# Later places for the steps between the products of a two-layer hybrid decoder, and the key latent's norm moved to GpSimd

## The chip, the cores and the metric

The kernel runs on one core of a Trainium2 chip. The metric is the device time of one execution in microseconds (us), as the median over several executions. Beside it stands one execution taken by the hardware profiler, from which all durations below come. The engines are TensorE (PE in the profile; PEld is its weight load), VectorE (DVE), ScalarE (ACT), GpSimd (POOL) and SyncE (SP), whose queue issues the DMAs. Each works through its own queue in order; semaphores tie the queues together.

## The reference

Two layers over 512 tokens of width 1024. In each, one projection of the normed input feeds three mixers side by side; their outputs are projected, gated, added and projected once more, and a squared-ReLU feed-forward of width 4096 follows. Cut to what matters here:

```python
# B: latent attention, 8 heads
q  = rmsnorm(cq, q_norm_g) @ w_uq           # query latent: 512 wide
kv = rmsnorm(ckv, kv_norm_g) @ w_ukv        # key latent: 256 wide
# A: chunked scan (4 chunks of 128 tokens), then a norm over each of 2 groups
y = ssd_chunked(xs * dt, dt * a, bm, cm) + d_skip * xs
y = rmsnorm((y * silu(z)).reshape(..., 2, 512), norm_g)
# C: gated delta rule, chunk after chunk
v_new = u - w @ state
o     = (q * exp(g)) @ state + attn @ v_new
state = state * exp(g_last) + (k * exp(g_last - g)).T @ v_new
```

`rmsnorm(x, g)` is `x * rsqrt(mean(x * x) + eps) * g`.

## The kernel before

**Products.** Nearly all the time goes into matrix products with both sides split into a high and a low part (`whi`/`wlo`, `xh`/`xl`), three matmuls for each pair of tiles (lines 200 to 202, `mm3`). ScalarE makes a weight's high part (L172), VectorE its low part (L173); the raw weights come by DMA into `wraw`, two buffers. `dense_F` (L204) gives outputs with features on the partitions: for each pair of k (128 rows of the weight each) it goes through the column tiles, and for each of them through the two k. A product over 1024 rows and 256 columns is 48 matmuls of 512 columns.

**Order.** The program is written down stage by stage, and a planner builds each engine's queue from it: what comes earlier in the program goes first when its inputs are ready by the planner's own costs. Two helpers bend that order on the matmul queue. `place` (L162) notes the last matmul of each k and column tile of a product under a key such as `((ly, "k", 2), 3, 0)`: product, k, column tile. `behind` (L155) makes an instruction follow the matmul noted under a key. It is a lower bound in the queue's order and no semaphore; the planner may still put the instruction later. With it the small matmuls and transposes of the mixers are laid between the matmuls of a big product that doesn't depend on them.

**The stages that the change touches**, in each of the two layers:

- *First stage and attention.* `front` (L397) computes the key latent `ck_tok` (four tiles of 128 tokens by 256), the rotary key and the step sizes. `query_latent` (L531) computes the query latent in two halves. `latent` (L509) squares the key latent on ScalarE, computes the factor (`rsq`, L276: one step on VectorE and a power on GpSimd, L278), scales the four tiles on VectorE (L519), transposes them on TensorE (L524) and splits them. It is called behind the second half, L565. The sums of the query latent's squares are matmuls with a column of ones (L568). Then for each pair of heads come the query product (four k, three column tiles: 36 matmuls, L600), the key and value products and the softmax.
- *Scan.* `ssd_group` (L734) runs for two groups over four chunks t: decays by DMA, L784 (within the chunk), L795 (from the state), L802 (state update), the squares' sums L816. At the end the norm's factors are transposed (L820), written to DRAM and read back on all partitions. These steps lie between matmuls of the attention's output product, with tag `(ly, 1, dp, "g")` for its gate half and `(ly, 1, dp, "y")` for the other.
- *Delta rule.* `gdn_unit` (L996) runs for two units u of four heads over four chunks t. For each t: L1044 (queries by keys), L1055 (keys by the state), L1058 on VectorE, L1061 (`pw`), L1066 on VectorE and L1072 on ScalarE, L1075 (`pS`, the state update), L1082, L1085 (`po`), L1092, the output norm (L1101 to L1113). At the end the output is transposed (L1118). Unit 0's steps lie between the matmuls of unit 1's query and value products (`(ly, "k", 2)`, `(ly, "v", 4)`, `(ly, "v", 6)`), unit 1's between those of the output projection. `pw_place`, `pg_place` and `end_place` (L1033 to L1035) hold the places. L1024 transposes a value tile behind its convolution.

PSUM has four banks for products (`acc`), three for small work (`sm`) and one more (`yt`).

Of the kernel before, what the change touches and what calls it, by code (L numbers as in the profile page):

```python
# [10 lines left out]
F32 = mybir.dt.float32  # L11
# [4 lines left out]
ALU = mybir.AluOpType  # L16
# [4 lines left out]
P = 128  # L21
# [34 lines left out]
def hybrid_kernel(ctx, tc, a, out, depth=2, taps=None):  # L56
# [326 lines left out]
    for ly in range(depth):  # L383
# [125 lines left out]
        def latent(pl, tok, width, gi, nm):  # L509

            nk = width // P
            ss = mk(sp, [P, T], F32, "lss")
            for t in range(T):
                jk = mk(ml, [P, width], F32, "pn3", 2)
                act.activation(jk, tok[t], AF.Square, accum_out=ss[:, t : t + 1])
            rs = mk(sp, [P, T], F32, "lrs")
            rsq(rs, ss, 1.0 / width, EPS)
            for t in range(T):
                dve.tensor_scalar(tok[t], tok[t], rs[:, t : t + 1], None, ALU.mult)  # L519
            hs, ls = hilo_tags(pl, nm, nk)  # L520
            for k in range(nk):
                ps = sm_bank()
                for t in range(T):
                    pe.transpose(ps[:, t * P : (t + 1) * P], tok[t][:, k * P : (k + 1) * P], ident)  # L524
                split_gain(hs[k], ls[k], ps, col(gi + k))
            return hs, ls
# [23 lines left out]

        query_latent(0)
# [15 lines left out]
        for t in range(T):  # L567
            pe.matmul(ps[:, t : t + 1], cq_sq[0][:, t * P : (t + 1) * P], ones[:, 0:1], start=True, stop=True)  # L568
# [13 lines left out]
        for hp in range(4):  # L582
# [17 lines left out]
            *pq, pp = dense_F(q_weights(), tiles(384), 512, cqh, cql)  # L600
# [133 lines left out]
        def ssd_group(g, yh, yl):  # L734
# [34 lines left out]
            for t in range(T):  # L769
# [11 lines left out]
                for c in range(4):  # L781
                    for i in range(2):
                        h = 2 * c + i
                        x = pe.matmul(py[64 * i : 64 * i + 64, c * P : (c + 1) * P], xd[:, t, h * 64 : (h + 1) * 64], e2[h // 4][:, h % 4, :], start=True, stop=True)  # L784
                        if t == 0:
                            behind(((ly, 1, 2 * g, "g"), 2, 0), x)
# [29 lines left out]
                pe.matmul(pss[:, t : t + 1], sq[:, 0], ones[:, 0:1], start=True, stop=True)  # L816
# [3 lines left out]
            behind(((ly, 1, 2 * g, "y"), 6, 0), pe.transpose(ps[:T, :P], rs, ident))  # L820
# [175 lines left out]
        def gdn_unit(u, kT, ork, cc, cd, Yt, yh, yl):  # L996
# [20 lines left out]
            for i in range(2):  # L1017
                for j, pj in enumerate(dense_F(weights(w_in, O_GV + (4 * u + 2 * i) * P, 256, D), tiles(256), D, xh, xl, tag=(ly, "v", 4 * u + 2 * i))):
                    h = 2 * i + j
                    vf = mk(br, [P, S], F32, "ft4", 2)  # L1020
                    gconv_silu(pj, 8 + 4 * u + h, vf)
                    ps = sm_bank()
                    for t in range(T):
                        pe.transpose(ps[:, t * P : (t + 1) * P], vf[:, t * P : (t + 1) * P], ident)  # L1024
                    dve.tensor_tensor(v[:, :, h * P : (h + 1) * P], ps.rearrange("p (t n) -> p t n", t=T),
                                      bc_last(ork[:, i, :], P), ALU.mult)
# [6 lines left out]
            pw_place = (seq[0], 3, 0), (seq[0], 5, 1), (seq[1], 1, 0)  # L1033
            pg_place = (seq[0], 5, 0), (seq[0], 7, 1)
            end_place = (seq[2], 1, 0) if u == 0 else (seq[2], 5, 0)  # L1035
            st = None
            for t in range(T):
# [30 lines left out]
                if t < T - 1:  # L1068
# [5 lines left out]
                    for i in range(2):  # L1074
                        pe.matmul(pS[:, i * 256 : (i + 1) * 256], ktok[i][:, t, :], vd[:, i * 256 : (i + 1) * 256], start=True, stop=True)  # L1075
# [8 lines left out]
                for h in range(4):  # L1084
                    x = pe.matmul(po[:, h * P : (h + 1) * P], pt_[:, h, :], vn[:, h * P : (h + 1) * P], start=True, stop=True)  # L1085
                    if t == T - 1:
                        behind((seq[1], 1, 1), x)
# [373 lines left out]
```

## Time and profile before

| | |
|---|---|
| median of 3 runs | 2291.31 us (2291.30 to 2293.06) |
| the profiled execution | 2290.89 us, of which the span from first to last instruction is 2289.1 us |
| PE busy | 2264.0 us, 99% of the span |
| DVE busy | 1647.4 us, 72% |
| ACT busy | 1202.8 us, 53% |
| POOL busy | 58.7 us, 3%, 75 instructions |
| DMA | 244.23 MB, 107 GB/s on the mean |
| clock granted to TensorE | 0.998 |

How to read the profile. A row of a group has line, engine, operation, tiles written and read, shapes and count, then its busy time, the mean of one in ns, and the idle time of its engine just before, with what ended it. A row of the order of time has its start in us from the span's start, its duration, engine, line and tiles; in square brackets is the idle time before it and what ended that. A row of the waits has who waited for whom, then idle time in total, times, and the longest. Matmuls overlap in the array, so a matmul's duration is longer than the distance to the next one's start.

### The profile page before, as it was taken

The numbers are of one execution on the slowest core, as the hardware profiler recorded it, in microseconds if no ns is written. First come the engines' busy times: TensorE is split into PE (matmuls) and PEld (weight loads), VectorE is DVE, ScalarE is ACT, GpSimd is POOL, SyncE is SP. The second block draws the span as 40 slices with busy tenths as digits, with TensorE's granted clock in tenths as the row PEclk, the third lists the DMA queues.
The fourth block names the chain that finished last, engine by engine and source line by source line (L and its number), as shares of the span: only waits on it lengthen the run. The fifth ranks groups of instructions, "written<-read, shape, count | busy, mean of one in ns | idle before, by whom it ended". The sixth has DMA issues, their size and how long they took to land.

```text
span 2289.1 us, 32304 instructions
## 1 busy us (share of the span) xinstructions
PE 2264.0 (99%) x11822; PEld 1866.7 (82%) x11822; DVE 1647.4 (72%) x3258; ACT 1202.8 (53%) x2508; POOL 58.7 (3%) x75
## 2 busy tenths in 40 slices
PE   9999999999999999999999999999999999999998
PEld 8888787888878888888888887878888887888886
DVE  7776567876676778767867775668757667778668
ACT  6766744333444465554657667443335435645545
POOL 0000000000000000000000000000001000000000
PEclk9999999999999999999999999999999999999999
DMA  4223633452225143233132236344422241432231
GB/s 144 81 74 102 193 102 120 123 150 76 77 74 172 59 148 111 92 109 105 52 100 78 77 104 199 96 119 140 129 76 82 65 170 52 166 108 99 89 111 47
DMA packets 220176, 244.23 MB, mean 107 GB/s; under 512 B 34272, under 2 KB 172528, under 8 KB 220016
## 3 DMA queue, kind: packets, MB, share of 16 engines
q1 hardware_dynamic: 220016, 242.16, 34.6%
q8 instruction: 93, 1.52, 0.3%
q14 instruction: 67, 0.55, 0.1%
HBM read 225.66 MB, written 11.74 MB: 104 GB/s over the span
## 4 chain that ended last, share of the span: by engine, by line
PE 91%; DVE 3%; ACT 2%; POOL 1%; DMA 1%; issue 0%; DVEq 0%; POOLq 0%; ACTq 0%; SPq 0%
PE acc L200 23%; PE acc L202 23%; PE acc L201 23%; PE sm L200 3%; PE sm L202 3%; PE sm L201 3%; DVE wlo L173 1%; PE sm L784 1%; PE sm L682 1%; PE sm L1085 1%; PE sm L1075 1%; PE yt L698 1%; ACT whi L172 1%; PE sm L662 1%; PE sm L659 0%
## 5 line engine op out<-in xcount | busy, mean ns | idle before, releaser
L173 DVE TENSOR_TENSOR wlo<-wraw,whi 128x512 fp32r<-128x512 f32 (+1 forms) x536 | 365.0, 686 | 344.0 <-ACT whi L172 333.8
L172 ACT CAST whi<-wraw 128x512 fp32r<-128x512 f32 (+1 forms) x536 | 329.5, 618 | 534.0 <-PE acc L201 367.1
L200 PE MATMUL acc<-xh,whi 128*128 128x512 f32 (+1 forms) x1344 | 524.5, 391 | 0.0
L201 PE MATMUL acc<-xl,whi 128*128 128x512 f32 (+1 forms) x1344 | 521.8, 388 | 0.0
L202 PE MATMUL acc<-xh,wlo 128*128 128x512 f32 (+1 forms) x1344 | 519.8, 387 | 0.0
L202 PEld LDWEIGHTS acc<-xh,wlo 128*128 128x128 f32 x1344 | 252.5, 188 | 48.8
L200 PEld LDWEIGHTS acc<-xh,whi 128*128 128x128 f32 x1344 | 252.5, 188 | 48.1 <-ACT xh L273 0.4
L201 PEld LDWEIGHTS acc<-xl,whi 128*128 128x128 f32 x1344 | 253.1, 188 | 47.3 <-DVE xl L274 0.7
L172 ACT CAST whi<-wr 128x512 fp32r<-128x512 f32 x168 | 104.3, 621 | 107.9 <-PE acc L201 47.7
L200 PE MATMUL acc<-yh,whi 128*128 128x512 f32 x384 | 151.5, 398 | 0.0
L201 PE MATMUL acc<-yl,whi 128*128 128x512 f32 x384 | 150.8, 393 | 0.0
L202 PE MATMUL acc<-yh,wlo 128*128 128x512 f32 x384 | 150.4, 392 | 0.0
L173 DVE TENSOR_TENSOR wlo<-wr,whi 128x512 fp32r<-128x512 f32 x168 | 113.2, 686 | 35.5 <-ACT whi L172 34.7
L723 DVE SCALAR_TENSOR_TENSOR ckl<-acc,pc,ckl 128x511 f32<-128x511 f32 (+2 forms) x168 | 121.1, 744 | 20.7 <-ACT ckl L719 13.0
L200 PEld LDWEIGHTS acc<-yh,whi 128*128 128x128 f32 x384 | 71.5, 188 | 16.7 <-ACT yh L273 2.3
L202 PEld LDWEIGHTS acc<-yh,wlo 128*128 128x128 f32 x384 | 72.2, 188 | 14.6
L201 PEld LDWEIGHTS acc<-yl,whi 128*128 128x128 f32 x384 | 72.2, 188 | 14.1
L200 PE MATMUL acc<-whi,xh 128*128 128x512 f32 (+1 forms) x208 | 79.9, 386 | 0.0
L201 PE MATMUL acc<-wlo,xh 128*128 128x512 f32 (+1 forms) x208 | 79.1, 380 | 0.0
L202 PE MATMUL acc<-whi,xl 128*128 128x512 f32 (+1 forms) x208 | 78.7, 381 | 0.0
L486 ACT ACTIVATE eE<-eE,cum 128x128 f32<-128x128 f32 x192 | 62.6, 391 | 28.6 <-DMA eE<-d_c 24.5
L1201 DVE TENSOR_TENSOR h<-h,acc 128x512 f32<-128x512 f32 x120 | 77.0, 680 | 0.1
(462 smaller groups left out, 4535.6 us busy)
## 6 DMA issues: line engine op xcount, KB each, us to landing
wraw<-in_w_in_dram SPq DMA_DIRECT2D x144, 512.0 KB, 3.6
wraw<-in_w_up_dram SPq DMA_DIRECT2D x64, 512.0 KB, 3.6
wr<-in_w_down_dram SPq DMA_DIRECT2D x32, 1024.0 KB, 5.3
eE<-d_c SPq DMA_DIRECT2D x48, 256.0 KB, 4.4
wraw<-in_w_mla_out_dram SPq DMA_DIRECT2D x16, 512.0 KB, 4.4
eE<-d_e SPq DMA_DIRECT2D x32, 256.0 KB, 3.1
wraw<-in_w_ssd_out_dram SPq DMA_DIRECT2D x16, 512.0 KB, 3.3
wraw<-in_w_gdn_out_dram SPq DMA_DIRECT2D x16, 512.0 KB, 3.4
```

Of the source, the lines that this page charges most:

```text
L172: act.copy(hi, raw)
L173: dve.tensor_tensor(lo, raw, f32(hi), ALU.subtract)
L200: pe.matmul(o, ah, bh, start=start, stop=False, skip_group_check=more)
L201: pe.matmul(o, ah, bl, start=False, stop=False, skip_group_check=more)
L202: return pe.matmul(o, al, bh, start=False, stop=stop, skip_group_check=more)
L486: act.activation(o[:, i], o[:, i], AF.Relu, scale=-1.0, bias=cum[:, t, h0 + i : h0 + i + 1])
L662: pe.matmul(o, qps[j][:, tok], kps[:, :n], start=False, stop=False)
L682: pe.transpose(ps[:, n : n + P], pn[t][:, kb * P : (kb + 1) * P], ident)
L698: pe.matmul(o, v_h, th[:, c : c + w], start=kb == 0, stop=False)
L723: dve.scalar_tensor_tensor(acc[:, d:], ps[:, : S - d], taps_[3 - d], acc[:, d:], ALU.mult, ALU.add)
L784: x = pe.matmul(py[64 * i : 64 * i + 64, c * P : (c + 1) * P], xd[:, t, h * 64 : (h + 1) * 64], e2[h // 4][:, h % 4, :], start=True, stop= ...
L1201: dve.tensor_tensor(hs_, hs_, ps[t], op)
```

## The change

It has five parts.

- `latent_norm` takes the squares, the factor and the scaling of the key latent out of `latent` and runs them before the first half of the query latent. The four scalings go from VectorE to GpSimd, and the squares' scratch tiles from the tag `pn3` to `yl6` and `yl7`.
- The key latent's eight transposes are laid behind k = 1, tile 2 of head pair 0's query product, the query latent's sums behind k = 3, tile 2; for this the product gets a tag.
- In the scan, the last chunk's L784 and the sums of chunks 2 and 3 get places in the half `"y"` of the output product, and the factors' transpose goes from that half to the next gate half.
- In unit 1 of the delta rule, the transposes of its first two value tiles get places in the next value product.
- In both units the places of `pw` (t = 2 and 3), `pg`, `po` and (unit 0) of the last transposes are later, and the state updates of t = 1 and t = 2 get places, `ps_place`.

No matmul is added or taken away. The diff:

```diff
--- before.py
+++ after.py
@@ -506,22 +506,25 @@
                             dve.tensor_tensor(mixed[d], mixed[d], tg[j], ALU.add)
 
 
-        def latent(pl, tok, width, gi, nm):
-
-            nk = width // P
+        def latent_norm(tok, width):
+
             ss = mk(sp, [P, T], F32, "lss")
             for t in range(T):
-                jk = mk(ml, [P, width], F32, "pn3", 2)
+                jk = mk(lp, [P, width], F32, f"yl{6 + t % 2}")
                 act.activation(jk, tok[t], AF.Square, accum_out=ss[:, t : t + 1])
             rs = mk(sp, [P, T], F32, "lrs")
             rsq(rs, ss, 1.0 / width, EPS)
             for t in range(T):
-                dve.tensor_scalar(tok[t], tok[t], rs[:, t : t + 1], None, ALU.mult)
+                pool.tensor_tensor(tok[t], tok[t], rs[:, t : t + 1].to_broadcast([P, width]), ALU.mult)
+
+        def latent(pl, tok, width, gi, nm):
+
+            nk = width // P
             hs, ls = hilo_tags(pl, nm, nk)
             for k in range(nk):
                 ps = sm_bank()
                 for t in range(T):
-                    pe.transpose(ps[:, t * P : (t + 1) * P], tok[t][:, k * P : (k + 1) * P], ident)
+                    behind(((ly, "q", 0), 1, 2), pe.transpose(ps[:, t * P : (t + 1) * P], tok[t][:, k * P : (k + 1) * P], ident))
                 split_gain(hs[k], ls[k], ps, col(gi + k))
             return hs, ls
 
@@ -548,6 +551,7 @@
             dve.tensor_tensor(ta, ta, sw_, ALU.add)
             return ta
 
+        latent_norm(ck_tok, 256)
         query_latent(0)
         ps = sm_bank()
         for t in range(T):
@@ -565,7 +569,7 @@
         ckh, ckl = latent(lp, ck_tok, 256, g_kv, "ck")
         ps = sm_bank()
         for t in range(T):
-            pe.matmul(ps[:, t : t + 1], cq_sq[0][:, t * P : (t + 1) * P], ones[:, 0:1], start=True, stop=True)
+            behind(((ly, "q", 0), 3, 2), pe.matmul(ps[:, t : t + 1], cq_sq[0][:, t * P : (t + 1) * P], ones[:, 0:1], start=True, stop=True))
         q_rs = mk(sp, [P, T], F32, "qrs")
         rsq(q_rs, ps[:, :T], 1.0 / 512, EPS)
 
@@ -597,7 +601,7 @@
                         dve.tensor_tensor(pv(lo), rv[:, :, P:], f32(pv(hi)), ALU.subtract)
                         yield k0 + k, hi.unsqueeze(1), lo.unsqueeze(1)
 
-            *pq, pp = dense_F(q_weights(), tiles(384), 512, cqh, cql)
+            *pq, pp = dense_F(q_weights(), tiles(384), 512, cqh, cql, tag=(ly, "q", hp))
 
             def head_tiles(pss, nm, c=None):
                 res = []
@@ -782,8 +786,8 @@
                     for i in range(2):
                         h = 2 * c + i
                         x = pe.matmul(py[64 * i : 64 * i + 64, c * P : (c + 1) * P], xd[:, t, h * 64 : (h + 1) * 64], e2[h // 4][:, h % 4, :], start=True, stop=True)
-                        if t == 0:
-                            behind(((ly, 1, 2 * g, "g"), 2, 0), x)
+                        if t in (0, T - 1):
+                            behind(((ly, 1, 2 * g, "g"), 2, 0) if t == 0 else ((ly, 1, 2 * g, "y"), 3, 0), x)
                 y = xf[:, :, tok]
                 dve.tensor_tensor(y, y, c4(py), ALU.add)
                 if t > 0:
@@ -813,11 +817,13 @@
                 act.activation(sq, zt, AF.Square)
                 dve.tensor_tensor(sq[:, 0:2], sq[:, 0:2], sq[:, 2:4], ALU.add)
                 dve.tensor_tensor(sq[:, 0], sq[:, 0], sq[:, 1], ALU.add)
-                pe.matmul(pss[:, t : t + 1], sq[:, 0], ones[:, 0:1], start=True, stop=True)
+                x = pe.matmul(pss[:, t : t + 1], sq[:, 0], ones[:, 0:1], start=True, stop=True)
+                if t > 1:
+                    behind(((ly, 1, 2 * g, "y"), 4 * t - 5, 0), x)
             rs = mk(sp, [P, T], F32, "srs")
             rsq(rs, pss[:, :T], 1.0 / 512, EPS)
             ps = sm_bank()
-            behind(((ly, 1, 2 * g, "y"), 6, 0), pe.transpose(ps[:T, :P], rs, ident))
+            behind(((ly, 1, 2 * g + 1, "g"), 1, 0), pe.transpose(ps[:T, :P], rs, ident))
             rsT = mk(br, [T, P], F32, "gk", 2)
             act.copy(rsT, ps[:T, :P])
             sync.dma_start(d_r[g].rearrange("(t p) -> t p", p=P), rsT)
@@ -1021,7 +1027,9 @@
                     gconv_silu(pj, 8 + 4 * u + h, vf)
                     ps = sm_bank()
                     for t in range(T):
-                        pe.transpose(ps[:, t * P : (t + 1) * P], vf[:, t * P : (t + 1) * P], ident)
+                        x = pe.transpose(ps[:, t * P : (t + 1) * P], vf[:, t * P : (t + 1) * P], ident)
+                        if u == 1 and i == 0:
+                            behind(((ly, "v", 6), 5, j), x)
                     dve.tensor_tensor(v[:, :, h * P : (h + 1) * P], ps.rearrange("p (t n) -> p t n", t=T),
                                       bc_last(ork[:, i, :], P), ALU.mult)
             silu_T(br, O_GZ + 512 * u, gz)
@@ -1030,9 +1038,10 @@
             ss = mk(sp, [P, T, 4], F32, "gos", 2)
             g_, y_ = ((ly, 2, i // 2, "gy"[i % 2]) for i in range(2))
             seq = [(ly, "k", 2), (ly, "v", 4), (ly, "v", 6)] if u == 0 else [g_, y_, (ly, 2, 1, "g")]
-            pw_place = (seq[0], 3, 0), (seq[0], 5, 1), (seq[1], 1, 0)
-            pg_place = (seq[0], 5, 0), (seq[0], 7, 1)
-            end_place = (seq[2], 1, 0) if u == 0 else (seq[2], 5, 0)
+            pw_place = (seq[0], 3, 0), (seq[0], 7, 0), (seq[1], 2, 0)
+            pg_place = (seq[0], 5, 1), (seq[1], 0, 1)
+            ps_place = (seq[0], 5, 0), (seq[1], 0, 0)
+            end_place = (seq[2], 7, 0) if u == 0 else (seq[2], 5, 0)
             st = None
             for t in range(T):
                 tok = slice(t * P, (t + 1) * P)
@@ -1072,7 +1081,9 @@
                             act.activation(hv(vd)[:, h], hv(pw)[:, h], AF.Copy, scale=cd[:, t, h : h + 1])
                     pS = sm_bank()
                     for i in range(2):
-                        pe.matmul(pS[:, i * 256 : (i + 1) * 256], ktok[i][:, t, :], vd[:, i * 256 : (i + 1) * 256], start=True, stop=True)
+                        x = pe.matmul(pS[:, i * 256 : (i + 1) * 256], ktok[i][:, t, :], vd[:, i * 256 : (i + 1) * 256], start=True, stop=True)
+                        if t > 0:
+                            behind(ps_place[t - 1], x)
                     sn = mk(br, [P, 512], F32, "st", 2)
                     if t == 0:
                         act.copy(sn, pS)
@@ -1084,7 +1095,7 @@
                 for h in range(4):
                     x = pe.matmul(po[:, h * P : (h + 1) * P], pt_[:, h, :], vn[:, h * P : (h + 1) * P], start=True, stop=True)
                     if t == T - 1:
-                        behind((seq[1], 1, 1), x)
+                        behind((seq[1], 2, 1), x)
                 o = mk(br, [P, 512], F32, "wk3")
                 if t > 0:
                     pq = sm_bank()
```

## The prediction

> **What bounds the kernel now.** I read the page first (parts 1 and 4), then the waits of the matmul queue, then the order of time around the longest of them.
>
> ```profile
> span 2289.1 us, 32304 instructions
> PE 2264.0 (99%) x11822; PEld 1866.7 (82%) x11822; DVE 1647.4 (72%) x3258; ACT 1202.8 (53%) x2508; POOL 58.7 (3%) x75
> ...
> PE 91%; DVE 3%; ACT 2%; POOL 1%; DMA 1%; issue 0%; DVEq 0%; POOLq 0%; ACTq 0%; SPq 0%
> ```
>
> TensorE is busy 99% of the span, and the change takes no matmul away and adds none. So all that it can win is time in which the matmul queue stands at a wait. Those waits are few:
>
> ```profile
> PE sm L1075 <- ACT wk L1072: 3.1, 4, 0.8
> PE sm L524 <- DVE yh L519: 2.0, 2, 1.2
> PE acc L200 <- ACT whi L172: 1.5, 2, 0.8
> ...
> PE yt L816 <- DVE wk L815: 1.1, 4, 0.5
> PE sm L1024 <- DVE ft L282: 1.0, 2, 0.5
> ...
> PE yt L1118 <- DVE tok L1113: 0.7, 2, 0.3
> ```
>
> The columns are idle time in total, times, longest. Five of these rows (L1075, L524, L816, L1024, L1118) stand at instructions that the diff moves: 3.1 + 2.0 + 1.1 + 1.0 + 0.7 = 7.9 us in 14 waits. The idle time is not all that a wait costs, as the order of time shows:
>
> ```profile
> 592.29 1.05 PE L1061 MATMUL sm<-tok,tok 128*128 128x128 f32 x8
> 593.10 0.48 PE L200 MATMUL acc<-xh,whi 128*128 128x512 f32 x1
> ...
> 594.33 0.39 PE L202 MATMUL acc<-xh,wlo 128*128 128x512 f32 x1
> 594.55 0.39 PE L200 MATMUL acc<-xh,whi 128*128 128x512 f32 x1
> 595.72 0.70 PE L1075 MATMUL sm<-wk,kt 128*128 128x256 f32 x2 [0.78 <-ACT wk L1072]
> ```
>
> Undisturbed, one product follows the other after 594.55 - 594.33 = 0.22 to 0.23 us (I use 0.227), although each is shown 0.39 long: they overlap by 0.16. The product before L1075 took 595.72 - 594.55 = 1.17 us to the next start: 0.94 lost, against 0.78 idle. So I add 0.16 for each wait: 14 x 0.16 = 2.2, and the five rows are worth **10.1 us**.
>
> Some delays are too short to show as idle time, and are read only from start to start:
>
> ```profile
> 604.59 0.40 PE L200 MATMUL acc<-xh,whi 128*128 128x512 f32 x1
> 604.93 0.70 PE L1075 MATMUL sm<-wk,kt 128*128 128x256 f32 x2
> ```
>
> ```profile
> 633.57 0.47 PE L201 MATMUL acc<-xl,whi 128*128 128x512 f32 x1
> 634.00 0.66 PE L1024 MATMUL sm<-ct,ft 128*128 128x128 f32 x4
> ```
>
> ```profile
> 261.28 0.40 PE L202 MATMUL acc<-yh,wlo 128*128 128x512 f32 x1
> 261.75 0.27 PE L820 MATMUL sm<-ct,srs 128*4 128x128 f32 x1
> ```
>
> 0.34 - 0.23 = 0.11 at the state update of t = 2 (four units in all), 0.43 - 0.23 = 0.20 at the second value tile (once a layer), 0.47 - 0.23 = 0.24 at the transposed factors of group 0 (once a layer): 0.44 + 0.40 + 0.48 = **1.3 us**. The most that these edits can win by removing waits is thus 10.1 + 1.3 = **11.4 us**.
>
> **The change part by part.** A place names a product: in the wide products, a pair of k gives six matmuls for column tile 0 and six for tile 1. So (3,0) is behind the 18th of 48, (5,0) the 30th, (5,1) the 36th, (7,0) the 42nd, (2,0) the 15th, (0,0) the 3rd. In the query product, (1,2) is the 18th of 36 and (3,2) the last. A place is a lower bound.
>
> *Key latent.* Before, its eight transposes come late in the query product and wait; in layer 0:
>
> ```profile
> 51.79 0.39 PE L200 MATMUL acc<-cqh,whi 128*128 128x512 f32 x1
> ...
> 59.58 0.39 PE L202 MATMUL acc<-cqh,wlo 128*128 128x512 f32 x1
> 60.85 1.23 PE L524 MATMUL sm<-ct,yh 128*128 128x128 f32 x8 [0.88 <-DVE yh L519]
> ```
>
> From 59.58 to 60.85 1.27 - 0.23 = 1.04 are lost (0.88 idle + 0.16); with layer 1 it is 2.0 + 2 x 0.16 = 2.3, within the 10.1. After, the squares and the scaling start when the first stage's last copy is done, and the transposes are due near 51.79 + 18 x 0.227 = 55.9 or later:
>
> ```profile
> 30.28 0.37 ACT L404 COPY yh<-acc 128x256 f32<-128x256 f32 x1
> ...
> 56.91 0.42 ACT L515 ACTIVATE pn<-yh 128x256 f32<-128x256 f32 x1
> ...
> 57.45 0.42 ACT L515 ACTIVATE pn<-yh 128x256 f32<-128x256 f32 x1
> ```
>
> Four squares go by 0.54 each (57.45 - 56.91): 30.6 + 2.2 = 32.8. The factor's step on VectorE, the power on GpSimd and the hand-overs between them take some 2 us more (59.07 to 60.44 for its last part below). So the four multiplications have from about 35 to 55.9, 21 us, **5.2 us each**. Their cost on GpSimd is in no row; the nearest are these:
>
> ```profile
> L278 POOL TENSOR_TENSOR lrs<-lrs,nhalf 128x4 f32<-128x4 f32 x2 | 2.0, 1017 | 68.6 <-DVE lrs L277 68.6
> L1008 POOL TENSOR_TENSOR grq<-gss,nhalf 128x8 f32<-128x8 f32 x4 | 6.6, 1641 | 205.6 <-DVE gss L1006 205.6
> L910 POOL MEMSET tok<- 128x1024 f32 x2 | 1.9, 960 | 0.0
> 59.07 0.17 DVE L277 TENSOR_SCALAR lrs<-lss 128x4 f32<-128x4 f32 x1 [1.14 <-ACT pn L515]
> 60.44 1.14 DVE L519 TENSOR_SCALAR yh<-yh,lrs 128x256 f32<-128x256 f32 x4 [1.20 <-POOL lrs L278]
> ```
>
> The fill writes 1024 elements in 0.96 us, 0.94 ns each: 0.24 us for 256 is the lower end. A power costs (1641 - 1017)/4 = 156 ns an element: 40 us for 256 is the upper end. A multiplication reads two operands and writes one with no function behind it, so I take the end of the fill, three times over: 0.7 us each, 2.9 in all, well inside 21. Then the whole 2.3 us goes. VectorE loses the 1.14 us of L519; it isn't the bound, so this is worth nothing. The squares on ScalarE (2.2 us) lie in the first query half, where the weights are split ahead; cost nothing. If that cover were gone, 2.2 us a layer. What is late next: the sums of the query latent, now behind the query product's last matmul; they need only run, 0.8 us, as now.
>
> By the Trainium skill (GPSIMD Engine Reference, Elementwise — side-by-side cycle accounting) a two-operand operation takes about 2.6 cycles an element at 1.2 GHz; as an estimate from that page, 0.55 us for 256 elements, and the sum would be the same. No run here shows it yet.
>
> *Scan of the first mixer.* L784 of the last t goes from the 13th product to the 18th, the sums L816 of t = 2 to the 18th and of t = 3 to the 42nd, the factors' transpose L820 from the 39th to the 6th of the next gate product. L816 waited at most 0.5 + 0.16 us, about three products; it gets six to eight more. L820 gets twelve products (2.7 us) behind its sums, where five and the 0.24 lost (1.4 us) were enough. So 1.1 + 4 x 0.16 + 0.48 = 2.2 us go. Behind L820 wait a copy on ScalarE and two DMAs on SP, and their result is read only after the last attention product, a whole product later: no cost.
>
> *Unit steps of the third mixer.* For t = 1, the multiplication L1061 stays at the 18th, and the state update L1075 goes from seven products behind it to twelve: 593.10 + 0.09 + 12 x 0.227 = 595.9, just past the 595.72 at which its input came. What ends that wait is on VectorE:
>
> ```profile
> 592.54 0.16 DVE L277 TENSOR_SCALAR gms<-gms 128x4 f32<-128x4 f32 x1
> ...
> 594.25 0.16 DVE L1110 SCALAR_TENSOR_TENSOR gms<-gms,grt 128x4 f32<-128x4 f32 x1 [0.90 <-POOL gms L278]
> 594.32 0.68 DVE L1066 TENSOR_TENSOR wk<-sm,gcc 128x512 f32<-128x512 f32 x1
> ```
>
> L1066 stands behind L1110, which waits for GpSimd's power, and ScalarE's L1072 behind L1066. The change leaves this; it gives TensorE work meanwhile. For t = 2 it becomes nine products (42nd to the 3rd of the next) where seven lost 0.11. So L1075 gives 3.1 + 4 x 0.16 + 0.44 = 4.2 us. On SP, two loads of the other unit wait for L1085, which moves along by 8 x 0.227 - 0.94 - 0.11 = 0.8 us for t = 2:
>
> ```profile
> 597.77 9.55 SPq L1041 DMA_DIRECT2D eE<-d_e  x2
> 610.16 0.38 SPq L179 DMA_DIRECT2D wraw<-in_w_in_dram  x1
> ```
>
> The weights behind them are issued 610.16 - 607.32 = 2.8 us after the second load, so nothing there is later.
>
> *Value tiles and unit 0's end.* L1024 goes to the 30th and 36th product (from about the 25th), L1118 to the 42nd (from the 34th). Their waits with the 0.16 and the 0.40 are 1.0 + 0.7 + 4 x 0.16 + 0.40 = 2.7 us. Here I don't count all. Both wait for a VectorE that is busy nearly throughout with the convolutions, and the waits removed ahead bring TensorE there earlier than VectorE. The loss given back lies between nothing and the whole 2.7; I take the middle, **1.4 us**.
>
> The sum: 2.3 + 2.2 + 4.2 + 2.7 = 11.4, less 1.4 = **10.0 us**. Against the profiled execution (2290.89 us, the span of 2289.1 and 1.8 around it) that gives 2280.9. The median, 2291.31, lies 0.42 above that execution: **2281.3 us**.
>
> **The rivals.**
>
> *Later places only move the waits.* The steps of a unit form one chain over t, and unit 1's must end before the products on its output:
>
> ```profile
> 695.45 1.03 PE L1092 MATMUL sm<-st,ft 128*128 128x256 f32 x4
> 705.87 0.60 PE L1118 MATMUL yt<-ct,tok 128*128 128x128 f32 x4
> 701.56 0.34 DVE L1113 SCALAR_TENSOR_TENSOR tok<-tok,gms,wk 128x128 f32<-128x128 f32 x1
> ```
>
> From L1092 to the end of L1113 are 6.5 us; L1118 comes 10.4 after L1092. With L1085 behind the 21st product instead of the 12th, 33 products, 7.5 us and L1092's own 0.9, remain: 1.9 us of room. If the chain slips by more, or the planner puts other VectorE work ahead, a wait of about the old size returns at the next step. Half the gain: 2291.3 - 5 = **2286.3**. For it: VectorE at 72% and the 0.90 us in which it stands at L1110. Against it: the rows above leave room at nearly each place. Chance 0.22.
>
> *GpSimd is too slow* (slower than before). Place: the transposes in the query product, in both layers; the matmul queue waits there with all products behind it. From 5.2 us a multiplication on, TensorE waits; from 5.2 + (10.0 + 4.6)/(2 x 4) = 7.0 us on, the kernel is over 0.2% slower. At 10 us each: 2 x (40 - 21) - 10 = +28, **2319**; at the power's rate, 2 x (160 - 21) - 10 = +268, 2559. For it: every two-operand row of GpSimd here costs above 0.5 us for one to eight elements. Against it: those rows are powers, and the fill is 150 times cheaper an element. Chance 0.12, what else may turn out slower included.
>
> By the Trainium skill (SBUF — State Buffer, Who interferes with whom) a VectorE instruction with two SBUF inputs and a GpSimd instruction that reads SBUF exclude each other, and the second waits for the first. No run here shows it yet. By that rule VectorE would lose at most the 2.9 us of the four multiplications a layer; TensorE loses nothing of it as long as the weights split ahead outlast it (four buffers of twelve products, 2.7 us each), and 2 x 2.9 = 5.8 us, 2287.1, if none were ahead.
>
> **How the numbers follow.** Forecast 0.66, moved waits 0.22, slow GpSimd 0.12. 0.2%, 4.6 us, is about what a measurement can tell from no change: faster is below 2286.7. The forecast and 0.08 of the moved waits lie there: 0.74; 0.14 of the moved waits and 0.01 of the third: 0.15 the same; 0.11 slower. All 11.4 us gone, and two more from rows that I didn't count, is 2278; moved waits reach to 2290. Range 2278 to 2290; some 0.16 lies above, 0.04 below.
>
> **What would show it.** Right: L524 and L816 gone from the waits of the matmul queue, L1075 under 1 us in total, L1024 and L1118 together about 0.8 us, GpSimd's multiplications under 2 us each and done before 50 us; the stretches outside these places unchanged. Wrong: L524 waiting for GpSimd, a new row above 1 us in those waits, L1118 of unit 1 waiting, or products waiting for L172's casts in the two stages.

## The result and the profile after

| | before | after |
|---|---|---|
| median, first measurement (11 runs each) | 2292.24 us | 2286.60 us (2283.81 to 2288.98) |
| ratio after to before, 95% interval | | 0.9978 (0.9969 to 0.9986) |
| the profiled execution | 2290.89 us | 2284.80 us |
| median, measured again later (e7) | 2291.81 us (22 runs) | 2283.84 us (6 runs, 2283.11 to 2287.62) |
| ratio of that, 95% interval | | 0.9967 (0.9956 to 0.9979) |

The kernel became faster by 5.6 us in the first measurement, and by 8.0 in the second. The forecast was 2281.3, 10 us under the kernel before. The direction was right and the time lies within the range; the forecast of 10 us was nearly twice what the first measurement gave. The two measurements of the changed kernel differ by 2.8 us, so a part of it that is worth less than that is read below from its waits, and not from the medians.

The first two lines of the page after, and the waits of the matmul queue after (idle time in total, times, longest):

```profile
span 2283.0 us, 32306 instructions
PE 2260.8 (99%) x11822; PEld 1867.7 (82%) x11822; DVE 1648.8 (72%) x3250; ACT 1202.1 (53%) x2508; POOL 64.9 (3%) x83
```

```profile
PE sm L752 <- DVE ft L282: 2.0, 2, 1.6
PE acc L200 <- ACT pn L539: 1.9, 1, 1.9
...
PE sm L1084 <- ACT wk L1081: 1.0, 4, 0.3
...
PE yt L1129 <- DVE yl L274: 0.8, 2, 0.4
```

Lines have moved: L1072 and L1075 are L1081 and L1084, L1085 is L1096, L1118 is L1129, L1066 and L1110 are L1075 and L1121, L784 is L788, L816 and L820 are L820 and L824, L536 is L539. The transposes of the key latent (2.0 us before), the sums (1.1) and the value tiles (1.0) are gone from the list, as forecast, and the state update has fallen from 3.1 to 1.0. The last transposes haven't gained: they waited 0.7 us for L1113 and now wait 0.8 for another step, L274. And two rows of about 2 us stand there that the kernel before had not at all (L752) or with a tenth of it:

```profile
PE acc L200 <- ACT pn L536: 0.2, 1, 0.2
```

L539, which squares the query latent on ScalarE, is an instruction that the diff doesn't touch; the bank that it reads can take the next product only when it has read it. L752 transposes a conv output of the scan's second group, which the diff doesn't touch either. So the question is what makes these two, and why the state update still waits.

### The profile page after: what moved, and what is told of

The parts are those of the page before. It is cut to its first block, busy times and chain, and to the rows that moved or that the text cites. A ratio compares the mean times of both kernels' runs of the same rounds, so it can differ in the third digit from the quotient of the medians.

```text
span 2283.0 us, 32306 instructions
## 1 busy us (share of the span) xinstructions
PE 2260.8 (99%) x11822; PEld 1867.7 (82%) x11822; DVE 1648.8 (72%) x3250; ACT 1202.1 (53%) x2508; POOL 64.9 (3%) x83
## 5 line engine op out<-in xcount | busy, mean ns | idle before, releaser
L200 PEld LDWEIGHTS acc<-xh,whi 128*128 128x128 f32 x1344 | 252.5, 188 | 48.9 <-ACT whi L172 0.6
L486 ACT ACTIVATE eE<-eE,cum 128x128 f32<-128x128 f32 x192 | 62.6, 391 | 30.8 <-DMA eE<-d_c 26.8
```

What stands on the lines that cost most here:

```text
L200: pe.matmul(o, ah, bh, start=start, stop=False, skip_group_check=more)
L486: act.activation(o[:, i], o[:, i], AF.Relu, scale=-1.0, bias=cum[:, t, h0 + i : h0 + i + 1])
```

## The experiments

Each was timed beside the kernel before on the same chip, in four sets; the kernels of one set share its runs of the kernel before (medians 2291.82 us for e1 to e3, 2291.81 for e4 to e7, 2291.40 for e8 to e11, 2291.47 for e12 and e13).

### The key latent: who should scale it (theories A and B)

What stands ahead of the new wait at L539? First GpSimd, then VectorE, each in the order of time after:

```profile
34.38 3.21 POOL L518 TENSOR_TENSOR yh<-yh,lrs 128x256 f32<-128x256 f32 x4
```

```profile
34.67 1.10 DVE L140 SCALAR_TENSOR_TENSOR qh<-qh,qh 128x512 f32<-128x512 f32 x1
35.70 0.67 DVE L432 SCALAR_TENSOR_TENSOR spe<-spv 128x96 f32<-128x96 f32 x1
36.29 0.83 DVE L137 TENSOR_SCALAR qh<-qh 128x512 f32<-128x512 f32 x1
37.05 0.61 DVE L444 TENSOR_SCALAR spv<-spv 128x96 f32<-128x96 f32 x1
```

Four multiplications on GpSimd, and beside them four VectorE steps that are each about 0.4 us longer than the same steps elsewhere. **Theory A**: the two engines exclude each other there, and the delay reaches TensorE by another way than the weights. **Theory B**: it is the order, squares and factor ahead of the rotary tables, that makes VectorE late. Two kernels put the scaling on another engine and leave the order of the matmul queue as it is.

```diff
-                pool.tensor_tensor(tok[t], tok[t], rs[:, t : t + 1].to_broadcast([P, width]), ALU.mult)
+                act.activation(tok[t], tok[t], AF.Copy, scale=rs[:, t : t + 1])
```

> The changed kernel with the key latent's four multiplications on ScalarE instead of GpSimd; the matmul queue's order and SP's are the same. Theory A, GpSimd blocks VectorE: at 34 to 37 us four VectorE steps took 1.66 us longer beside the four multiplications, and through ScalarE's queue that reaches the query product as a new wait (acc, ended by L539, 1.92 us idle in layer 0). Then these VectorE steps are back at 0.68, 0.25, 0.42 and 0.20 us, the wait at 53 us falls below 0.5 us, and the time is 1.7 us under the changed kernel's, about 2283.1 us in a profiled execution. Theory B, the order is the cause (squares and factor ahead of the rotary tables delay VectorE and ScalarE): the wait stays above 1.5 us and the time within 0.5 us of the changed kernel's.

Measured: 2282.24 us (2281.71 to 2283.18), ratio 0.9959 (0.9946 to 0.9971), the profiled execution 2282.70. The VectorE steps of e1_act_scale:

```profile
35.35 0.68 DVE L140 SCALAR_TENSOR_TENSOR qh<-qh,qh 128x512 f32<-128x512 f32 x1
35.95 0.25 DVE L432 SCALAR_TENSOR_TENSOR spe<-spv 128x96 f32<-128x96 f32 x1
36.12 0.42 DVE L137 TENSOR_SCALAR qh<-qh 128x512 f32<-128x512 f32 x1
36.46 0.20 DVE L444 TENSOR_SCALAR spv<-spv 128x96 f32<-128x96 f32 x1
```

The difference is 0.42 + 0.42 + 0.41 + 0.41 = 1.66 us. The way to TensorE is read in two engines' order of time, first after, then e1_act_scale:

```profile
51.96 0.62 ACT L564 CAST kph<-mix 128x512 fp32r<-128x512 f32 x1 [1.61 <-DVE mix L551]
...
54.88 0.60 ACT L539 ACTIVATE pn<-acc 128x512 f32<-128x512 f32 x1
...
55.53 0.50 PE L200 MATMUL acc<-cqh,whi 128*128 128x512 f32 x1 [1.92 <-ACT pn L539]
```

```profile
51.12 0.62 ACT L564 CAST kph<-mix 128x512 fp32r<-128x512 f32 x1 [0.51 <-DVE mix L551]
...
54.03 0.60 ACT L539 ACTIVATE pn<-acc 128x512 f32<-128x512 f32 x1
...
54.69 0.50 PE L200 MATMUL acc<-cqh,whi 128*128 128x512 f32 x1 [0.26 <-ACT pn L539]
```

ScalarE stands at L564, which needs the rotated key from VectorE (L551), and L539 is behind it in ScalarE's queue. The product needs the bank that L539 reads. TensorE's wait falls from 1.92 to 0.26 us, 1.66 us: what the four steps had lost. (The query product itself starts at 52.09 in after and at 52.90 in e1_act_scale; against that start, L564 comes 0.84 + 0.81 = 1.65 us earlier.) In that stretch VectorE's steps stand in the same order in both kernels. Theory A holds in place and size of the wait; B is out.

> The changed kernel with the four multiplications on VectorE, as before the change, but at their new place; the matmul queue's order is the same. Theory A: VectorE loses 1.14 us to its own four multiplications where it lost 1.66 us to GpSimd, so the wait ended by L539 in layer 0 shrinks from 1.92 to about 1.4 us and the time is 0.5 us under the changed kernel's. Theory B: the wait stays at 1.9 us or grows by 1.1 us, since VectorE has more to do ahead of the rotary tables.

```diff
-                pool.tensor_tensor(tok[t], tok[t], rs[:, t : t + 1].to_broadcast([P, width]), ALU.mult)
+                dve.tensor_scalar(tok[t], tok[t], rs[:, t : t + 1], None, ALU.mult)
```

Measured: 2282.84 us, ratio 0.9961 (0.9949 to 0.9974); the wait ended by L539 is 0.2 us, where A expected 1.4 and B 1.9 or more. Both were wrong here, for this kernel changes VectorE's order too. In e1_act_scale three steps L442 of the step sizes run at 48.07 to 48.9 us, ahead of the rotated key (L551 at 50.40). Here L551 runs at 49.63, and the first L442 comes behind it:

```profile
52.02 0.55 DVE L442 SCALAR_TENSOR_TENSOR spe<-spe,spq 128x96 f32<-128x96 f32 x2
```

So this run doesn't separate the two theories; e1_act_scale does.

Why did layer 1 not show the wait? Busy time of the engines after in the same stretch of each layer:

```profile
32.00:54.00 22.00, 21.61 (x98) 17.53 (x96) 21.27 (x50) 11.71 (x24) 4.71 (x5) 1.00 0.32 87
1160.00:1182.00 22.00, 22.00 (x108) 18.79 (x107) 16.26 (x41) 10.98 (x25) 3.83 (x5) 1.00 0.34 96
```

The columns are length, then PE, PEld, VectorE, ScalarE, GpSimd. In layer 0 VectorE computes the rotary tables there and is busy for 21.27 of 22.00 us. In layer 1 it has 5.7 us to spare. The two engines hold each other up in layer 1 too:

```profile
1167.40 2.81 POOL L518 TENSOR_TENSOR yh<-yh,lrs 128x256 f32<-128x256 f32 x4
```

```profile
1167.67 0.89 DVE L173 TENSOR_TENSOR wlo<-wraw,whi 128x512 fp32r<-128x512 f32 x1
1168.48 0.67 DVE L437 TENSOR_TENSOR sps<-sps,spe 128x96 f32<-128x96 f32 x1
```

In layer 1 of e1_act_scale these two take 0.68 and 0.26 us. But there L564 (at 1183.44) finds the rotated key ready, and no wait at L539 follows. That the spare time is the reason is read from these rows; no run fills it. The forecast went by VectorE's mean of 72% over the span.

The same question the other way round, with the first four hunks of the change alone (first with GpSimd, then with the line of e1_act_scale):

> The kernel before with the key latent's part of the change alone. By the forecast's term 2.3 us under the kernel before (ratio 0.9990). By theory A (1.7 us of it lost again in layer 0, another 0.5 us gained in layer 1 at the last head pair's waits): about 1.5 us under it, ratio 0.9993, and the wait ended by L539 at 53 us is there with 1.9 us idle; the wait at L748 (L752 in the changed kernel) is not there.

Measured: 2291.99 us, ratio 0.9999 (0.9990 to 1.0008): with GpSimd no gain is seen of the part by itself. The interval reaches from 2.3 us faster to 1.8 slower, so the forecast's 2.3 lies at its edge and theory A's 1.5 inside it. The wait at L539 is there with 1.9 us.

> The kernel before with the key latent's part alone, scaled on ScalarE instead of GpSimd. The forecast priced this part at 2.3 us; with GpSimd it measured nothing (ratio 0.9999). Theory A: with GpSimd's lock gone the part is worth its 2.3 us, less 0.2 us that remain at L539: about 2289.7, ratio 0.9991 (0.9986 to 0.9996), 1.7 us under the profiled time with GpSimd (less what the start adds by chance). Theory B: the part is worth nothing wherever the scaling runs, ratio 0.9997 or more.

Measured: 2289.71 us, ratio 0.9991 (0.9982 to 1.0000), as theory A had it, and the wait ended by L539 is 0.3 us. Forecast for the part: 2.3 us; on ScalarE 2291.40 - 2289.71 = 1.7; on GpSimd none. The intervals of e3 and e11 overlap, so the medians alone wouldn't show the difference; the wait does.

> The changed kernel once more, beside the others of this call, as their base and for its spread from execution to execution (2283.8 to 2289.0 so far, where the two kernels without GpSimd's multiplications spread over 1.5 and 2.1 us). Theory A says that the wait ended by L539 in layer 0 (1.92 us) is there again with 1.5 to 2.5 us, and the time is 3 to 4.5 us above e5. If that wait is mostly chance, it differs by over 1 us from the first profile.

Measured: 2283.84 us. The wait ended by L539 is there with 1.7 us, so it isn't chance. But the time is 0.9 us above e5's, not 3 to 4.5, and 1.6 above e1_act_scale's, where the first measurement had put it 3.9 above (each against the kernel before of its own set). So the price of GpSimd's scaling is known from the wait, 1.66 us, and only roughly from the time. The changed kernel spreads, and part of the spread is the other new row: here L752 is down to 0.5.

```profile
PE acc L200 <- ACT pn L539: 1.7, 1, 1.7
...
PE sm L752 <- DVE ft L282: 0.5, 1, 0.5
```

### The delta rule (theories E to H)

The last four hunks of the change alone, on the kernel before:

> The kernel before with the part of the change in the delta rule alone (places of the state updates, value tiles, unit 0's end). The forecast's terms for it are 4.2 + 1.3 = 5.5 us, so 2286.3 and a ratio of 0.9976. By the stage balance of the changed kernel (0.90 + 0.72 in layer 0, 0.83 + 0.72 in layer 1, 3.2 us) about 2288.6, ratio 0.9986; then L1084's waits are near 1.0 us in 4 and a wait of 0.8 us at L1129 is there, both as in the changed kernel.

Measured: 2288.43 us, ratio 0.9985 (0.9976 to 0.9994): 3.4 us, where the forecast had 5.5, at the edge of the interval. The waits are those of the changed kernel (L1078 is L1084 there):

```profile
PE sm L1078 <- ACT wk L1075: 1.0, 4, 0.3
...
PE yt L1123 <- DVE yl L274: 0.8, 2, 0.4
```

So, by the waits, this part's shortfall is its own. Where it is, the order of time after shows on TensorE, ScalarE and VectorE:

```profile
596.92 0.59 PE L1084 MATMUL sm<-wk,kt 128*128 128x256 f32 x2
597.76 0.70 PE L1084 MATMUL sm<-wk,kt 128*128 128x256 f32 x2 [0.24 <-ACT wk L1081]
598.29 1.05 PE L1096 MATMUL sm<-wk,eE 128*128 128x128 f32 x8
```

```profile
596.04 0.89 ACT L1081 ACTIVATE wk<-sm,gcd 128x128 f32<-128x128 f32 x3 [3.55 <-DVE wk L1075]
596.81 0.62 ACT L172 CAST whi<-wraw 128x512 fp32r<-128x512 f32 x1
597.32 0.39 ACT L1081 ACTIVATE wk<-sm,gcd 128x128 f32<-128x128 f32 x1
```

```profile
595.25 0.16 DVE L1121 SCALAR_TENSOR_TENSOR gms<-gms,grt 128x4 f32<-128x4 f32 x1 [0.90 <-POOL gms L278]
595.33 0.68 DVE L1075 TENSOR_TENSOR wk<-sm,gcc 128x512 f32<-128x512 f32 x1
```

The state update needs four copies L1081, and the first pair of its matmuls only part of them. The forecast took the time of the first pair. The fourth copy ends 597.32 + 0.39 - 596.04 = 1.67 us after the first begins, so the second pair now waits. Before, on TensorE, six matmuls of L1085 stood between the pairs:

```profile
596.26 0.83 PE L1085 MATMUL sm<-wk,eE 128*128 128x128 f32 x6
596.92 0.60 PE L1075 MATMUL sm<-wk,kt 128*128 128x256 f32 x2
```

And all of it starts 0.90 us late, since VectorE stands at L1121. The forecast saw that stand and left it. The next edit, on top of e1_act_scale, puts the step behind L1075 of t = 1, by an order on VectorE's queue alone:

```diff
-                dve.scalar_tensor_tensor(ms, ms, 0.5, rqt, ALU.mult, ALU.mult)
+                x = dve.scalar_tensor_tensor(ms, ms, 0.5, rqt, ALU.mult, ALU.mult)
+                if t == 0:
+                    behind(("vn", ly, u), x)
...
-                    dve.tensor_tensor(hv(vn), hv(pw), bc_last(cc[:, t, :], P), ALU.mult)
+                    x = dve.tensor_tensor(hv(vn), hv(pw), bc_last(cc[:, t, :], P), ALU.mult)
+                if t == 1:
+                    place(("vn", ly, u), x)
```

> The changed kernel with the key latent scaled on ScalarE (2282.2 us), and at t = 1 VectorE's multiplication L1075 ahead of the factor step L1121 that waits 0.90 us for GpSimd's power; no other engine's order changes. Theory E, that stand is what keeps a wait at L1084 for t = 1 after the change: L1075 starts at once behind L1070, the waits of 0.25 us inside L1084 go in all four units, and 4 x 0.27 = 1.1 us are won, 2281.1. Theory F, ScalarE's cast L172 between the third and the fourth L1081 keeps it: L1084's waits stay near 1.0 us in 4 and the time at 2282.2.

Measured: 2280.24 us (2279.05 to 2282.65), ratio 0.9950 (0.9937 to 0.9963). VectorE, ScalarE and TensorE in e8 (L1081, L1084 and L1096 are L1083, L1086 and L1098 here):

```profile
592.31 0.69 DVE L1075 TENSOR_TENSOR wk<-sm,gcc 128x512 f32<-128x512 f32 x1
593.19 0.16 DVE L1123 SCALAR_TENSOR_TENSOR gms<-gms,grt 128x4 f32<-128x4 f32 x1 [0.19 <-POOL gms L278]
```

```profile
593.81 0.63 ACT L172 CAST whi<-wraw 128x512 fp32r<-128x512 f32 x1
594.32 0.38 ACT L1083 ACTIVATE wk<-sm,gcd 128x128 f32<-128x128 f32 x1
```

```profile
594.85 1.02 PE L1086 MATMUL sm<-wk,kt 128*128 128x256 f32 x4
595.71 1.05 PE L1098 MATMUL sm<-wk,eE 128*128 128x128 f32 x8
```

From the first matmul of the state update to the first of the next step are 595.71 - 594.85 = 0.86 us, where after shows 598.29 - 596.92 = 1.37 (L1096 starts at 598.29). That is 0.51 a unit and 2.0 in four units, twice the expectation, which had taken the idle time for the loss. The median is 2.0 us under e1_act_scale's as well, but the same program once more (e13 below) is only 0.7 under it, so the gain is shown by the distances, which e13 repeats (0.87), and not by the times. ScalarE's cast is still between the third and fourth copy, so it isn't enough by itself to make the wait: theory F is out and E holds. Whether moving the cast instead would have done as well wasn't tried. The row of the state update is gone from the waits.

> The changed kernel with the key latent scaled on ScalarE, and unit 0's last splits L274 at high priority. Theory G, what is left of unit 0's end (0.54 + 0.22 us lost at L1129 a layer) is the one bank of these transposes, held until L274 has read it, and L274 stands behind other VectorE work: the waits at L1129 go and the time falls by up to 1.5 us, to 2280.7. Theory H, VectorE is what is short there and another wait comes in place of it (value tiles L1030, or casts): L1129's wait shrinks, a new one of the same size appears within 15 us, and the time stays within 0.4 us of 2282.2.

```diff
-                split_gain(yh[k], yl[k], ps, col(g_gdn))
+                with tc.high_priority() if u == 0 else nullcontext():
+                    split_gain(yh[k], yl[k], ps, col(g_gdn))
```

Measured: 2281.81 us, ratio 0.9955 (0.9942 to 0.9968).

```profile
PE yt L1129 <- DVE yl L274: 0.7, 2, 0.4
```

The wait at the first bank stays (VectorE's split is still behind a step of a convolution); the shorter one behind it went. 0.4 us by the median is within the spread. Neither theory is shown.

> Both edits together, as the best version so far. Theories E and G: 2282.2 - 1.1 - 1.5 = 2279.6; F and H: 2282.2. In between if one of the two holds.

Measured: 2280.38 us, ratio 0.9950 (0.9937 to 0.9963), as e8 alone; the last transposes still wait 0.8 us. E's gain is there, and nothing is seen of G's.

### The scan (theories C and D)

Undone in e2, all three; in e5 the first alone, in e6 the other two:

```diff
-                        if t in (0, T - 1):
-                            behind(((ly, 1, 2 * g, "g"), 2, 0) if t == 0 else ((ly, 1, 2 * g, "y"), 3, 0), x)
+                        if t == 0:
+                            behind(((ly, 1, 2 * g, "g"), 2, 0), x)
...
-                if t > 1:
-                    behind(((ly, 1, 2 * g, "y"), 4 * t - 5, 0), x)
...
-            behind(((ly, 1, 2 * g + 1, "g"), 1, 0), pe.transpose(ps[:T, :P], rs, ident))
+            behind(((ly, 1, 2 * g, "y"), 6, 0), pe.transpose(ps[:T, :P], rs, ident))
```

> The changed kernel with the scan's three places (last L784, sums, factors' transpose) as before the change. Theory C, these places delay SP's queue and with it weights and exchange tiles behind group 0 in layer 0, which makes the new wait at L752 (1.63 us idle at 296 us) and the one of 0.17 us at 285 us: both go, the sums' waits (1.1 us in 4) come back, layer 0's group 0 is some 1.2 us shorter, the other three groups together 2.5 us longer than in the changed kernel, total 1 to 1.5 us slower than the changed kernel, about 2286. Theory D, the wait at L752 comes from the slip in the attention stage ahead: it stays at 1 us or more, and the time is 2.5 us or more above the changed kernel's.

Measured: 2286.81 us, ratio 0.9976 (0.9967 to 0.9985); the span is 2285.1 us, 2.1 above the changed kernel's first profile and 3.6 above its second (e7, 2281.5). The wait at L752 is gone, and these are back:

```profile
PE yt L820 <- DVE wk L819: 1.0, 4, 0.4
```

So D is out: the slip ahead (the wait at L539, 1.8 us, is in this kernel too) doesn't make the wait at L752; the scan's later places do. In layer 0 that wait is 0.5 to 1.6 us in the nine profiles of kernels with all three places, and not there in the five without any (before, e2, e3, e4, e11). What the places are worth in all stays rough: 2.1 or 3.6 us by the spans, 0.6 or 3.0 by the medians (each against the kernel before of its set), depending on which measurement of the changed kernel is taken; the forecast's 2.2 lies among them. Two kernels undo one half each, on top of e1_act_scale (whose L752 waits 1.2 us):

> The changed kernel with the key latent scaled on ScalarE (2282.2 us), and of the scan's three places the one of the last chunk's L788 as before the change; sums and factors' transpose stay at the later places. Theory C1, the later L788 frees the exchange tiles late and so delays the loads behind it: the wait at L752 in layer 0 (1.19 us) goes, and the time is 0 to 1 us under 2282.2. Theory C2, the factors' DMAs that now come later in SP's queue delay the loads behind them: the wait at L752 stays above 0.8 us, and the four groups lose 0.2 to 0.4 us each in switches between products and small matmuls, 2283 to 2284 us.

> The same with L788's place kept and the sums and the factors' transpose at the places before the change. Theory C1: the wait at L752 stays near 1.2 us and the sums' waits (1.0 us in 4) are back, 2283.5 to 2284.5 us. Theory C2: the wait at L752 is below 0.3 us and SP issues the factors' two DMAs some 4 to 7 us earlier; the sums' waits are back, about 2282.5 us.

e5: 2282.94 us, ratio 0.9961 (0.9949 to 0.9974); e6: 2286.32 us, ratio 0.9977 (0.9968 to 0.9986), 1.8 us or more above either expectation. Waits of e5, then of e6:

```profile
PE sm L788 <- DVE eE L783: 0.7, 2, 0.4
```

```profile
PE yt L820 <- ACT eE L486: 1.2, 2, 0.9
...
PE yt L820 <- DVE wk L819: 0.9, 4, 0.4
...
PE sm L824 <- POOL srs L278: 0.6, 2, 0.3
```

The wait at L752 is 0.23 us in e5 (by the order of time) and nothing in e6, so neither half alone makes it as in e1_act_scale. Each has an effect of its own: without the later L788 its own wait for VectorE appears (0.7 us), without the later sums three waits with 2.7 us in all, of which the one for L486 (1.2) may be chance, for e13 below has it too. The place of L788 was priced at nothing in the forecast; it saves a wait that the sums' places uncover.

> The kernel of e8 (VectorE's step first, key latent on ScalarE; 2280.2 us) with group 0's two factor DMAs behind the loads of the second half of the decays in SP's queue, by one more copy of 4 x 128 on ScalarE; the matmul queue's order is the same. Theory C2, it is the place of these two DMAs among the decay loads that makes the wait at L752 in layer 0 (1.21 us in e8, 0.5 to 1.6 us in the other kernels with that order): it falls below 0.4 us, and the time is about 1 us under e8's in this call. Theory C3, the decay loads and stores are late by themselves, because the steps around them moved: the wait stays between 0.5 and 1.6 us and the time within 0.4 us of e8's.

```diff
             act.copy(rsT, ps[:T, :P])
+            if g == 0:
+                rsT, rs0 = mk(sp, [T, P], F32, "rst"), rsT
+                behind((ly, "decays"), act.copy(rsT, rs0))
...
-            act.activation(of, of, AF.Exp, scale=-1.0)
+            x = act.activation(of, of, AF.Exp, scale=-1.0)
+            if (t, h0) == (T - 1, 20):
+                place((ly, "decays"), x)
```

Measured: 2280.34 us, ratio 0.9949 (0.9936 to 0.9961).

```profile
PE sm L754 <- DVE ft L282: 1.2, 1, 1.2
```

L754 is L752 here. The factors' two DMAs start at 273.56 and 275.39 us, where e8 has 266.39 and 272.53; they now follow the delta rule's decays, and only two decay loads still come behind them. The wait is 1.2 us as in e8, so by the wait C2 falls. By the time it is less clear: 2280.34 is 1.2 under e13's, the same program as e8 in this kernel's own set, as C2 had it, but 0.1 above e8's own.

> The kernel of e8 once more, as the base of e12 in this call and for the spread of the wait at L752: under both theories that wait is between 0.5 and 1.6 us in layer 0, the waits at L1084 stay gone, and the time is 2279.5 to 2281 us.

Measured: 2281.54 us, ratio 0.9952 (0.9939 to 0.9966), just above the expected 2279.5 to 2281. The same program as e8 shows this, and L752 at 0.8:

```profile
PE yt L820 <- ACT eE L486: 1.3, 1, 1.3
```

ScalarE stands in its queue at the decay tiles' loads in all these profiles, and mostly longer with the later places. Before, then after:

```profile
276.08 1.28 ACT L486 ACTIVATE eE<-eE,cum 128x128 f32<-128x128 f32 x4 [2.31 <-DMA eE<-d_c]
```

```profile
278.24 1.28 ACT L486 ACTIVATE eE<-eE,cum 128x128 f32<-128x128 f32 x4 [2.98 <-DMA eE<-d_c]
...
296.31 0.62 ACT L172 CAST whi<-wraw 128x512 fp32r<-128x512 f32 x1 [2.08 <-DMA wraw<-in_w_in_dram]
```

The weights' casts stand in the same queue, and the next weights are loaded when the casts have freed their buffer. ScalarE's idle time at these loads in layer 0 (from 262 to 290 us) is 6.3 to 8.7 us in the nine profiles with all three places and 4.5 to 5.8 in the five without. But e5 idles 7.0 us there and L752 waits only 0.23, where e12 idles 6.3 and L752 waits 1.2. So the reading fits most profiles and not all, no run tests it, and why the two halves must come together stays open. So does the rest of the spread of the changed kernel.

## Why the prediction was half right

- **The bound.** Right: what was won lies in waits of the matmul queue. Of the five rows three went and the state update's shrank to 1.0; the last transposes' kept its size, ended by another step. The forecast's own sign of being wrong, "a new row above 1 us in those waits", came twice.
- **The key latent: this step failed.** The forecast says of GpSimd's multiplications "well inside 21. Then the whole 2.3 us goes", and of the lock "TensorE loses nothing of it as long as the weights split ahead outlast it". Their length was indeed no matter: 3.21 us for four, done at 37.6 us. But the loss came neither by the transposes nor by the weights. It came by the rotary tables, ScalarE's queue and a PSUM bank, 1.66 us in layer 0. The wait at L539 shows it: 1.7 to 1.9 us in the four profiles that scale on GpSimd (after, e7, e2, e3), 0.25 to 0.32 in the ten that have the new order and scale elsewhere. In e3 the part won nothing by the median, in e11 1.7, each within some 2 us. The lock was in the text, with VectorE's loss bounded by 2.9 us a layer; what failed is that only one way from VectorE to TensorE was looked at, and that VectorE's load was read from the mean of 72% instead of from that stretch (21.27 of 22.00 us).
- **By the Trainium skill (SBUF — State Buffer, Who interferes with whom)** a VectorE instruction in a two-port mode, or one with two SBUF inputs beside a GpSimd read, and a GpSimd instruction exclude each other, and the one that issues second waits for the whole of the first. The trace agrees that they hold each other up: in layer 0 each VectorE step is longer by 0.41 to 0.42 us. That each waited for one whole instruction is not shown: no row has GpSimd's multiplication undisturbed, and in layer 1 the steps are longer by 0.21, 0.41, 0.30 and 0.30 us.
- **The rivals.** "Later places only move the waits" (2286.3) and the lock's rival (2287.1) lie nearest to the first measurement, and each has a part in it: the second pair's wait and L752 are moved waits, and the lock reached TensorE, though in one layer only and not by the weights.
- **GpSimd's cost.** Forecast 0.7 us each; beside VectorE's steps it is 0.80 in layer 0 (3.21 for four) and 0.70 in layer 1 (2.81). The 0.55 that the prediction estimates beside its own has no undisturbed row here to be held against. The rival "too slow" needed 7.0 and is out.
- **The delta rule: this term was mis-sized.** The mechanism was right, the size too big: 5.5 forecast, 3.4 in e4. The term "L1075 gives 3.1 + 4 x 0.16 + 0.44 = 4.2 us" was read from the first pair of matmuls. The second pair kept 0.51 us a unit, 2.0 in all, which e8 then won. Of the 0.44 for t = 2, unit 0 kept its share: in after L1084 starts 0.38 and 0.37 us behind the last product there, in the two layers, and 0.23 in unit 1, so 0.29 stayed. The half given back at the value tiles and unit 0's end was about right: of 2.7 us, 1.5 remain, 0.54 + 0.21 a layer at L1129 by the distances in the order of time. So 4.2 - 2.0 - 0.29 + 2.7 - 1.5 = 3.1 us by the distances, near e4's 3.4.
- **The scan.** Forecast 2.2; between 0.6 and 3.6 with and without the places (e2), so its size is not settled. It is a balance of terms that the forecast didn't have: a gain at L788, a loss at L752 that changes from execution to execution. "No cost" behind L820 missed the wait at L752; by e12's wait it isn't the two DMAs that cost it, and what does stays open.
- **The sum.** By the parts' own measurements 0 + 3.4 + 2.1 = 5.5 us, against 5.6 in the first measurement. That they meet so closely is luck: each part is known to some 2 us at best, and the second measurement gave 8.0. With the scaling on ScalarE the changed kernel is at 2282.24, 0.9 above the forecast; with VectorE's step first too it is at 2280.24 (ratio 0.9950, 0.9937 to 0.9963) and, measured again, at 2281.54 (0.9952, 0.9939 to 0.9966), 10 to 11 us under the kernel before.

## What to carry to other kernels

Work moved to an idle engine isn't free when it holds up a busy one, as GpSimd held up VectorE here: look at the load of the busy engine in that stretch, and follow its output through every in-order queue to TensorE, not only along the path that is being mended. When a step with several inputs is given a place, take the time of its last input, and look at what fills the gap now. A term of a sum is tested best by a kernel with that part alone.

## What was not expected of the hardware

- One-input steps are held up by GpSimd as well as two-input ones: L137 (TENSOR_SCALAR, 128x512) 0.83 us instead of 0.42, L444 (TENSOR_SCALAR, 128x96) 0.61 instead of 0.20. In layer 0 the delay is the same whatever the length of the VectorE step, so short steps suffer most, in proportion; in layer 1 it is 0.21 to 0.41 us. The Trainium skill (SBUF — State Buffer, Who interferes with whom) exempts a VectorE instruction with at most one SBUF input unless it is in a two-port mode; whether these two were in one, no run here shows. Undisturbed, L137 takes 0.42 us where the two-input L140 of the same size takes 0.68.
- The same four multiplications took 3.21 us in layer 0, and there cost TensorE 1.66 us; in layer 1 they took 2.81 us and cost it no wait at that place.
- A program's waits change between executions by over 1 us: L752 1.6 and 0.5 us in two profiles of the changed kernel, and L820 none and 1.3 us in two of e8.
